# Two-layer gated trunk: feed-forward part with a right-side pool for the first gated block and every third weight slab

## The chip, the cores and the metric

The kernel runs on one NeuronCore of a Trainium2 chip. The metric is the device time of one execution in microseconds (us). The time before is the median of three runs, 2985.6 us. The page and the trace are of one further execution of the same kernel, taken by the profiler.

## What is computed

A decoder trunk of two layers on x of 1024 positions by 1024 channels, all in fp32. Of each layer, only the last lines concern the change (`attention_and_conv` stands for the rest):

```python
c_act = jax.nn.silu(c)
for l in range(2):
    mod = c_act @ ada_w[l] + ada_b[l]            # 6 vectors of 1024: shift, scale, gate, twice
    x = attention_and_conv(x, mod)
    h2 = rms_norm(x, norm2_g[l]) * (1.0 + scale2) + shift2
    f_gate, f_up = jnp.split(h2 @ w_ffn_in[l], 2, axis=-1)      # 1024 -> 2 x 2816
    x = x + (1.0 + gate2) * ((jax.nn.silu(f_gate) * f_up) @ w_ffn_out[l])   # 2816 -> 1024
return rms_norm(x, final_g)
```

## The kernel before

**Layout.** x is held transposed, eight tiles `xs[j]` of 128 channels by 1024 positions; positions are worked on in two halves of 512 (`HS`). Every operand of a matmul is split into two parts, hi and lo: ACT casts it to the matmul type (hi), and POOL or DVE subtracts hi from it (lo). One product of a 128 x 128 weight block with a 128 x 512 block is then three matmuls, hi by hi, hi by lo and lo by hi. `split_into` does the two steps; its subtraction runs on the engine that it is given, V for DVE or G for POOL.

**Feed-forward, first matrix.** It is worked in 22 groups (`Group`, FT = 22), one for each 128 columns of gate and of up. A group computes a 2 x 2 arrangement (two halves of the channels by two halves of the positions) by seven products instead of eight, each of 12 matmuls of 128 x 512. The seven right operands `MV[1]` to `MV[7]` (b1 to b7, each with h and l) are made once a layer: b1, b2, b3 in `normed`, and b4 to b7 from sums and differences of the halves of `xs` (lines 822 to 835). Each operand is four 128 x 512 blocks. The weights come as `wraw` and `fraw`, 512 KB each; sums of them are formed on DVE (lines 866 to 869, `s1`), and their split is on ACT and POOL (`wt`). The gated results go to DRAM, as `gf`. The first three groups are interleaved so that the products of b1 and b2 run while the other operands are being made; the third group's first half comes early (`r1e`).

**Second matrix.** `xs` is loaded again from `xm` (line 996), since the pool of the first `xs` was closed after the preparation. `gblock` loads four of the 22 `gf` tiles for one half of the positions as `gs` (line 970) and splits them into `gh` and `gl`; there are six blocks a half, five of four tiles and one of two. 48 slabs of weights follow (`wslab`: load at line 137, cast at 141, POOL's subtraction at 142), 24 for each half of the positions: a slab holds two columns of output by one block, 24 matmuls (lines 1017 to 1019). In layer 0 the second layer's `ada_w` is multiplied in the same stretch, 48 columns in two loads of 256 KB each (`ada_next`, `adraw`, line 987; its product on DVE is line 988); the tag `gs` has five buffers for gs, adraw and cb.

**What sets the order.** The instructions are written through a framework that puts them into an order of its own, from an estimate of each engine's time, and adds the waits. Pools of SBUF are stacks on a left and on a right side; a tile in a new pool waits for the readers of whatever lay there before. All loads and stores go through one queue, SP, in order: where one has to wait, those behind it wait too.

Of the kernel before, what the change touches and what calls it, by code (L numbers as in the profile page):

```python
# [9 lines left out]
F32 = mybir.dt.float32  # L10
# [3 lines left out]
ALU = mybir.AluOpType  # L14
# [4 lines left out]
P = 128  # L19
D = 1024  # L20
T = 1024
L = 2
KT = D // P
HF = 512
HEADS = 4
D_FF = 2816
FT = D_FF // P
# [34 lines left out]
def trunk(tc, a):  # L62
# [4 lines left out]
    def pool(name, bufs=1, side="left", **k):  # L67
        return tc.tile_pool(name=name, bufs=bufs, side=side, reuse_waits="tile", **k)
# [255 lines left out]
    def hunit(name, pl=None, tag="H", bufs=8):  # L324

        return (pl or hp).tile([P, 4, HF], F32R, tag=tag, name=name, bufs=bufs)
# [213 lines left out]
    for l in range(L):  # L540
# [240 lines left out]

        def split_into(hi, lo, src, E):
            S.copy(hi, src)  # L783
            E.tensor_tensor(lo, src, hi.bitcast(F32), op=ALU.subtract)  # L784

        HS = [slice(hf * HF, hf * HF + HF) for hf in range(2)]
        MV = {}

        def normed(hf, pb, j):

            p = {(0, 0): 1, (0, 1): 2, (1, 1): 3}.get((hf, j // 4))
            if p and p not in MV:
                MV[p] = [(hunit if hf else h2unit)(f"b{p}{n}") for n in "hl"]
            x = xs[j][:, HS[hf]]
            t = nt("ntt")
            V.scalar_tensor_tensor(t, x, acol[l][1][:, j:j + 1], pb, op0=ALU.mult, op1=ALU.mult)
            S.activation(x, t, AF.Identity, bias=modb[l][:, 24 + j:25 + j])
            if p:
                split_into(MV[p][0][:, j % 4, :], MV[p][1][:, j % 4, :], x, V if hf and j % 2 else G)

        pb = None
        for hf in range(2):
# [19 lines left out]
        for jj in range(4):  # L822
            a11, a12 = (xs[jj][:, h] for h in HS)
            a21, a22 = (xs[4 + jj][:, h] for h in HS)
            E = (V, G)[jj % 2]
            E.tensor_tensor(a11, a12, a11, op=ALU.subtract)
            E.tensor_tensor(a12, a22, a12, op=ALU.subtract)
            E.tensor_tensor(a22, a22, a11, op=ALU.subtract)
        for p, x0, h in ((6, 4, 1), (7, 0, 1), (5, 0, 0), (4, 4, 0)):
            MV[p] = [(h2unit if p == 4 else hunit)(f"b{p}{n}") for n in "hl"]  # L830
            for jj in range(4):
                x = xs[x0 + jj][:, HS[h]]
                if p == 4:
                    (G, V)[jj % 2].tensor_tensor(x, xs[4 + jj][:, HS[1]], x, op=ALU.subtract)
                split_into(MV[p][0][:, jj, :], MV[p][1][:, jj, :], x, V if jj % 2 else G)
        xpool.close()


        def bank(name):
# [5 lines left out]
        class Group:  # L845
# [9 lines left out]

            def load(self):
                r1 = wp.tile([P, D], F32, tag="wraw", name="wraw", bufs=2)
                r2 = F.tile([P, D], F32, tag="fraw", name="fraw", bufs=2)
                DQ.dma_start(r1, a["w_ffn_in"][l, self.f])
                DQ.dma_start(r2, a["w_ffn_in"][l, FT + self.f])  # L860
                self.a11, self.a12, self.a21, self.a22 = r1[:, 0:HF], r1[:, HF:D], r2[:, 0:HF], r2[:, HF:D]
# [72 lines left out]

        wtags = itertools.cycle(("wh", "wl"))
        banks = itertools.cycle((psct, p1, psct, p1, psct, pct, pmt, pmt))
        gs = [Group(f) for f in range(FT)]
        for g in gs[:2]:
            g.load()
# [7 lines left out]
        for g in gs[2:]:  # L947
            g.load()
            for p in (1, 2, 6, 7, 5, 3, 4)[2 if g is gs[2] else 0:]:
                g.product(p)  # L950
        fst.close()


# [1 line left out]
        xp = xpool.enter_context(pool(f"y{l}", side="right"))  # L955
        xs = [xp.tile([P, T], F32, tag=f"x{j}", name=f"x{j}") for j in range(KT)]
        gst = ExitStack()
        GP = gst.enter_context(pool("gbuf"))
        g2 = gcol[l][1]
        NB = (FT + 3) // 4  # L960

        def gblock(hf, b):
            if b == NB - 1:
                u = hunit("gt", GP, "G", 9)
                un = [u[:, 0:2, :], u[:, 2:4, :]]
            else:
                un = [hunit(f"g{n}") if b >= 3 + hf else hunit(f"g{n}", GP, "G", 9) for n in "hl"]
            for k in range(4 * b, min(4 * b + 4, FT)):
                t = GP.tile([P, HF], F32, tag="gs", name="gs", bufs=5)
                DQ.dma_start(t, gf[k][:, HS[hf]])  # L970
                split_into(un[0][:, k % 4, :], un[1][:, k % 4, :], t, V if k % 2 else G)
            return un

        if l + 1 < L:
            cs1 = GP.tile([P, D], F32, name="cs1", bufs=1)
            for h in HS:
                cb = GP.tile([P, HF], F32, tag="gs", name="cb", bufs=5)
                DQ.dma_start(cb, a["cb"][:, h])
                S.activation(cs1[:, h], cb, AF.Sigmoid)
                V.tensor_tensor(cs1[:, h], cs1[:, h], cb, op=ALU.mult)  # L980

        def ada_next(t):

            m2 = small("m2", 2)
            for h in range(2):
                raw = GP.tile([P, HF], F32, tag="gs", name="adraw", bufs=5)
                DQ.dma_start(raw, a["ada_w"][l + 1, t][:, HS[h]])
                V.scalar_tensor_tensor(raw, raw, 1.0, cs1[:, HS[h]], op0=ALU.mult, op1=ALU.mult,
                                       accum_out=m2[:, h:h + 1])
            m = modb[l + 1][:, t:t + 1]  # L990
            V.scalar_tensor_tensor(m, m2[:, 0:1], m2[:, 1:2], vcol(l + 1, t), op0=ALU.add, op1=ALU.add)
            ada_use(l + 1, t)

        gb = [[gblock(0, b) for b in range(NB)], []]
        for j in range(KT):
            DQ.dma_start(xs[j], xm[j])
        ada_t = iter(range(48 if l + 1 < L else 0))
        for hf in range(2):
            hs = HS[hf]
            Sq = nt("Sq")  # L1000
            for jq in range(2):
                js = range(4 * jq, 4 * jq + 4)
                pss = [(psct, psct, psct, pmt, pmt, p1, p1, pct)[j]("pfo") for j in js]
                last = hf and jq
                steps = [(b, q) for b in range(NB) for q in range(2)]
                if last:
                    steps = [(b, q) for q in range(2) for b in reversed(range(NB))]
                seen = [0, 0]
                for b, q in steps:
                    k0, k1 = 4 * b, min(4 * b + 4, FT)  # L1010
                    wh, wl = wslab(a["w_ffn_out"][l, js[2 * q]:js[2 * q] + 2, :, k0 * P:k1 * P], k1 - k0, nj=2)
                    bh, bl = gb[hf][b]
                    for jj in range(2):
                        ps = pss[2 * q + jj]
                        for k in range(k0, k1):
                            wc = slice((jj * (k1 - k0) + k - k0) * P, (jj * (k1 - k0) + k - k0 + 1) * P)
                            PE.matmul(ps, wh[:, wc], bh[:, k % 4, :], start=(not seen[q] and k == k0), stop=False)  # L1017
                            PE.matmul(ps, wh[:, wc], bl[:, k % 4, :], start=False, stop=False)  # L1018
                            PE.matmul(ps, wl[:, wc], bh[:, k % 4, :], start=False,  # L1019
                                      stop=(seen[q] == NB - 1 and k == k1 - 1))  # L1020
                    seen[q] += 1
                    for t in itertools.islice(ada_t, 3):
                        ada_next(t)
                    if hf == 0 and q == 1 and (b == 0 if jq == 0 else b < NB - 1):
                        gb[1].append(gblock(1, len(gb[1])))
                    if seen[q] == NB:
                        for j in js[2 * q:2 * q + 2]:
                            V.scalar_tensor_tensor(xs[j][:, hs], pss[j % 4], g2[:, j:j + 1], xs[j][:, hs],  # L1028
                                                   op0=ALU.mult, op1=ALU.add)
                            sum_sq(Sq, xs, hf, j)  # L1030
                            if l + 1 < L:
                                DQ.dma_start(xd[j][:, hs], xs[j][:, hs])
            pb = rstd_bcast(Sq, 1.0 / D, 1e-6, "prn")
            if l + 1 < L:
                hs_parts[hf] = norm_half(xs, hf, pb, acol[l + 1][0], modb[l + 1][:, 0:8], "h")
            else:
                for j in range(KT):
                    y = nt("y")
                    V.scalar_tensor_tensor(y, xs[j][:, hs], vec[:, FG + j:FG + j + 1], pb,  # L1039
                                           op0=ALU.mult, op1=ALU.mult)  # L1040
                    DQ.dma_start(a["out"][j][:, hs], y)
        gst.close()
    xpool.close()
    top.close()

# [55 lines left out]
```

## Time and profile before

| what | value |
|---|---|
| median of three runs | 2985.6 us (2981.32 to 2988.03) |
| profiled execution | 2990.07 us, span 2988.2 us, mean granted clock 0.965 |
| busy, of the span | PE 93%, DVE 61%, POOL 58%, ACT 39% |
| DMA | 353.92 MB, mean 118 GB/s |

The profile is read in stages, since a share of the whole span says little about any of them. In layer 0 the feed-forward's start is 793.30 to 873.50 us of the span, its steady groups run to 1251.30, the out part's first half to 1426.98 and the second half to 1550.10. In layer 1 the same borders are 2254.10, 2332.80, 2711.30 and, at the end of the out part, 2972.40.

### The profile page before, as it was taken

To read this page: it belongs to the slowest core of one execution; us is meant where nothing else is said; L and a number is where in the kernel's file an instruction comes from. 1 tells how busy PE (TensorE), PEld (TensorE's weight loads), DVE (VectorE), ACT (ScalarE), POOL (GpSimd) and SP (SyncE) were. 2 spreads that over 40 slices of the span, in tenths; PEclk is the share of its full clock that TensorE was granted. 3 is DMA by queue.
4 is the path that set the end of the run, shared out by engine and by line. 5 is a ranking of instruction groups with operands and counts; after the bars stand their busy time and mean duration, and the time that the engine had idled before them with its cause. 6 is when DMAs were issued, how large, how long until landed. Compare 5 with 4: busy or idle time off the path is not lost. (4 is left out here: it accounts for less than half of the span.)

```text
span 2988.2 us, 35455 instructions
## 1 busy us (share of the span) xinstructions
PE 2783.1 (93%) x12544; PEld 2284.7 (76%) x12544; DVE 1836.9 (61%) x2997; ACT 1158.0 (39%) x2059; POOL 1719.9 (58%) x1256
## 2 busy tenths in 40 slices
PE   3899999899979999889899999998997999998998
PEld 2688788777758888667788888886875788886886
DVE  8889976554574466589618989545446644443222
ACT  4246544343433333332322565435334233333321
POOL 6957745334686666554542776642457666666643
PEclk9999999989989999999999999998998999999999
DMA  7621222335232222388432122132451322225442
GB/s 272 229 83 65 71 78 85 113 102 194 100 110 88 78 85 85 112 277 287 158 121 89 64 75 78 56 107 85 141 201 68 119 85 85 85 78 180 136 121 93
DMA packets 151952, 353.92 MB, mean 118 GB/s; under 512 B 15328, under 2 KB 28000, under 8 KB 151776
## 3 DMA queue, kind: packets, MB, share of 16 engines
q1 hardware_dynamic: 151776, 351.67, 34.7%
q8 instruction: 99, 1.62, 0.2%
q14 instruction: 77, 0.63, 0.1%
HBM read 282.30 MB, written 69.30 MB: 118 GB/s over the span
## 5 line engine op out<-in xcount | busy, mean ns | idle before, releaser
L142 POOL TENSOR_TENSOR wl<-wraw,wh 128x1024 fp32r<-128x1024 f32 (+1 forms) x216 | 513.0, 2376 | 587.1 <-ACT wh L141 391.2
L141 ACT CAST wh<-wraw 128x1024 fp32r<-128x1024 f32 (+1 forms) x216 | 219.5, 1017 | 404.5 <-PE pfo L1018 186.7
L784 POOL TENSOR_TENSOR wt<-wraw,wt 128x512 fp32r<-128x512 f32 x172 | 247.7, 1441 | 169.6 <-ACT wt L783 169.5
L1017 PE MATMUL pfo<-gh,wh 128*128 128x512 f32 x640 | 256.1, 402 | 31.1 <-ACT gh L783 22.8
L151 PE MATMUL pg<-hl,wh 128*128 128x512 f32 x640 | 253.0, 397 | 16.9 <-DVE hl L536 16.8
L614 DVE SCALAR_TENSOR_TENSOR pc<-uc,vec,pc 128x512 f32<-128x512 f32 x348 | 261.1, 750 | 6.0
L150 PE MATMUL pg<-hh,wh 128*128 128x512 f32 x640 | 253.8, 401 | 9.1 <-ACT hh L535 8.9
L1018 PE MATMUL pfo<-gl,wh 128*128 128x512 f32 x640 | 254.3, 397 | 0.0
L1019 PE MATMUL pfo<-gh,wl 128*128 128x512 f32 x640 | 243.0, 399 | 8.7 <-POOL wl L142 8.6
L783 ACT CAST wt<-wraw 128x512 fp32r<-128x512 f32 x172 | 106.9, 622 | 310.2 <-PE pf L883 259.2
L609 POOL TENSOR_TENSOR uc<-uc,ct 128x512 f32<-128x512 f32 x120 | 139.0, 1158 | 57.5 <-ACT ct L608 56.8
L1017 PEld LDWEIGHTS pfo<-gh,wh 128*128 128x128 f32 x640 | 124.1, 194 | 60.9 <-ACT gh L783 23.7
L154 PE MATMUL pg<-hh,wl 128*128 128x512 f32 x640 | 168.7, 395 | 0.0
L443 ACT ACTIVATE e<-psc,nb 128x512 f32<-128x512 f32 (+2 forms) x192 | 110.5, 579 | 145.9 <-DVE nb L440 113.1
L1019 PEld LDWEIGHTS pfo<-gh,wl 128*128 128x128 f32 x640 | 123.3, 193 | 42.1 <-POOL wl L142 16.5
L151 PEld LDWEIGHTS pg<-hl,wh 128*128 128x128 f32 x640 | 121.0, 189 | 44.2 <-DVE hl L536 21.1
L150 PEld LDWEIGHTS pg<-hh,wh 128*128 128x128 f32 x640 | 121.8, 191 | 33.5 <-ACT hh L535 9.4
L1028 DVE SCALAR_TENSOR_TENSOR x<-pfo,gcol,x 128x512 f32<-128x512 f32 x32 | 23.7, 745 | 196.0 <-PE pfo L1019 195.5
L1018 PEld LDWEIGHTS pfo<-gl,wh 128*128 128x128 f32 x640 | 123.2, 192 | 25.9
L154 PEld LDWEIGHTS pg<-hh,wl 128*128 128x128 f32 x640 | 117.5, 188 | 23.3
L784 POOL TENSOR_TENSOR wt<-fraw,wt 128x512 fp32r<-128x512 f32 x88 | 118.7, 1349 | 26.9 <-ACT wt L783 26.9
L438 DVE TENSOR_REDUCE mx<-psc 128x1 f32<-128x512 f32 (+2 forms) x192 | 102.7, 549 | 23.8 <-PE psc L437 16.0
(324 smaller groups left out, 7652.3 us busy)
## 6 DMA issues: line engine op xcount, KB each, us to landing
wraw<-in_w_ffn_out_dram SPq DMA_DIRECT2D x80, 512.0 KB
wraw<-in_w_in_dram SPq DMA_DIRECT2D x72, 512.0 KB
adraw<-in_ada_w_dram SPq DMA_DIRECT2D x48, 512.0 KB
adraw<-in_ada_w_dram SPq DMA_DIRECT2D x96, 256.0 KB
fraw<-in_w_ffn_in_dram SPq DMA_DIRECT2D x44, 512.0 KB
wraw<-in_w_ffn_in_dram SPq DMA_DIRECT2D x44, 512.0 KB
gs<-gf SPq DMA_DIRECT2D x88, 256.0 KB
gd<-graw SPq DMA_DIRECT2D x64, 256.0 KB
```

The lines of the kernel that those rows point to most:

```text
L141: S.copy(wh, raw)
L142: G.tensor_tensor(wl, raw, wh.bitcast(F32), op=ALU.subtract)
L150: PE.matmul(ps, wh[:, wc], rhs(0, k, hf), start=(k == 0), stop=False)
L151: PE.matmul(ps, wh[:, wc], rhs(1, k, hf), start=False, stop=False)
L154: PE.matmul(ps, wl[:, wc], rhs(0, k, hf), start=False, stop=(k == nk - 1))
L443: S.activation(e[:, n0:n1], pss[b][:, 0:n1 - n0], AF.Exp, bias=nb, scale=0.125, accum_out=sx[:, 2 * b + c:2 * b + c + 1])
L609: G.tensor_tensor(acc, acc, t, op=ALU.add)
L614: E.scalar_tensor_tensor(pc if k + 1 < CONV_K else acc, u[:, k:k + HF], w, pc, op0=ALU.mult, op1=ALU.add)
L784: E.tensor_tensor(lo, src, hi.bitcast(F32), op=ALU.subtract)
L1017: PE.matmul(ps, wh[:, wc], bh[:, k % 4, :], start=(not seen[q] and k == k0), stop=False)
L1018: PE.matmul(ps, wh[:, wc], bl[:, k % 4, :], start=False, stop=False)
L1019: PE.matmul(ps, wl[:, wc], bh[:, k % 4, :], start=False, stop=(seen[q] == NB - 1 and k == k1 - 1))
```

## The change

- A pool `ffnr` (R) is opened on the right side when the first `xs` pool has been closed, and stays until the layer's end. It holds one buffer for the second slab of every third group (`rraw`), the hi and lo parts of one gated block (`G0`), and the five gs buffers; `cs1` uses rraw's place later. The G tag falls from 9 to 7 buffers.
- The first gated block of the first half, `gblock(0, 0)`, is written into the feed-forward groups, behind group FT - 4; `gblock` itself moves ahead of the groups.
- The reloads of `xs` from `xm` move from ahead of the out part's slabs to its first steps.
- `ada_next` is called once a step, where it was called three times.
- Of the preparation, every subtraction of the second half of the positions, the differences and their splits go to DVE, where they alternated between DVE and POOL.

```diff
@@ normed
-                split_into(MV[p][0][:, j % 4, :], MV[p][1][:, j % 4, :], x, V if hf and j % 2 else G)
+                split_into(MV[p][0][:, j % 4, :], MV[p][1][:, j % 4, :], x, V if hf else G)
@@ differences
-            E = (V, G)[jj % 2]
+            E = V
             E.tensor_tensor(a11, a12, a11, op=ALU.subtract)
             E.tensor_tensor(a12, a22, a12, op=ALU.subtract)
             E.tensor_tensor(a22, a22, a11, op=ALU.subtract)
...
-                    (G, V)[jj % 2].tensor_tensor(x, xs[4 + jj][:, HS[1]], x, op=ALU.subtract)
-                split_into(MV[p][0][:, jj, :], MV[p][1][:, jj, :], x, V if jj % 2 else G)
+                    V.tensor_tensor(x, xs[4 + jj][:, HS[1]], x, op=ALU.subtract)
+                split_into(MV[p][0][:, jj, :], MV[p][1][:, jj, :], x, V)
         xpool.close()
+        rst = ExitStack()
+        R = rst.enter_context(pool("ffnr", side="right"))
@@ Group.load
-                r2 = F.tile([P, D], F32, tag="fraw", name="fraw", bufs=2)
+                if self.f % 3 == 2:
+                    r2 = R.tile([P, D], F32, tag="rraw", name="rraw", bufs=1)
+                else:
+                    r2 = F.tile([P, D], F32, tag="fraw", name="fraw", bufs=2)
@@ gblock (moved ahead of the groups)
+            if b == NB - 1:
+                u = hunit("gt", GP[0], "G", 7)
+                un = [u[:, 0:2, :], u[:, 2:4, :]]
+            elif b == 0 and hf == 0:
+                un = [hunit(f"g{n}", R, "G0", 2) for n in "hl"]
+            elif b == 1 and hf == 1:
+                un = [hunit(f"g{n}", R, "G0", 2) for n in "hl"]
+            else:
+                un = [hunit(f"g{n}") if b >= 3 + hf else hunit(f"g{n}", GP[0], "G", 7) for n in "hl"]
+            for k in range(4 * b, min(4 * b + 4, FT)):
+                t = R.tile([P, HF], F32, tag="gs", name="gs", bufs=5)
@@ groups
             for p in (1, 2, 6, 7, 5, 3, 4)[2 if g is gs[2] else 0:]:
                 g.product(p)
+            if g.f == FT - 4:
+                gb = [[gblock(0, 0)], []]
@@ out part
-        gb = [[gblock(0, b) for b in range(NB)], []]
-        for j in range(KT):
-            DQ.dma_start(xs[j], xm[j])
+        gb[0] += [gblock(0, b) for b in range(1, NB)]
...
-                    for t in itertools.islice(ada_t, 3):
+                    for t in itertools.islice(ada_t, 1):
                         ada_next(t)
+                    if hf == 0 and jq == 0 and q == 0 and b >= 2:
+                        for j in range(2 * b - 4, 2 * b - 2):
+                            DQ.dma_start(xs[j], xm[j])
```

The order of both kernels shows what becomes of this on the engines. The lines of the changed file are a few higher: 864 and 865 are the loads of wraw and of fraw or rraw (859 and 860 before), 871 to 874 the weight sums (866 to 869), 957 the load of gs (970), 1000 that of adraw (987), 1037 that of x from xm (996).

First, DVE at the end of the preparation in layer 0; b4l is the lo part of the last operand, s1 the first weight sum of the third group. Before:

```order
L784 TENSOR_TENSOR b6l_7134<-x7_6416,b6h_7133 128x512
L784 TENSOR_TENSOR b4l_7164<-x7_6416,b4h_7163 128x512
L915 TENSOR_TENSOR u2_7202<-pf_7352,u2_7202 128x512
L919 TENSOR_TENSOR u3_7399<-pf_7386,u2_7202 128x512
L915 TENSOR_TENSOR u2_7220<-pf_7369,u2_7220 128x512
...
L892 TENSOR_TENSOR u2_7220<-u2_7220,c22_7458 128x512
L892 TENSOR_TENSOR c11_7277<-c11_7277,u3_7417 128x512
L866 TENSOR_TENSOR s1_7512<-fraw_7508 128x512
```

And with the change:

```order
L784 TENSOR_TENSOR b6l_7134<-x5_6414,b6h_7133 128x512
L784 TENSOR_TENSOR b5l_7154<-x0_6409,b5h_7153 128x512
L784 TENSOR_TENSOR b5l_7154<-x1_6410,b5h_7153 128x512
L784 TENSOR_TENSOR b5l_7154<-x2_6411,b5h_7153 128x512
L784 TENSOR_TENSOR b5l_7154<-x3_6412,b5h_7153 128x512
L784 TENSOR_TENSOR b6l_7134<-x6_6415,b6h_7133 128x512
L784 TENSOR_TENSOR b4l_7164<-x4_6413,b4h_7163 128x512
L784 TENSOR_TENSOR b6l_7134<-x7_6416,b6h_7133 128x512
L784 TENSOR_TENSOR b4l_7164<-x5_6414,b4h_7163 128x512
L784 TENSOR_TENSOR b4l_7164<-x6_6415,b4h_7163 128x512
L784 TENSOR_TENSOR b4l_7164<-x7_6416,b4h_7163 128x512
L871 TENSOR_TENSOR s1_7515<-rraw_7511 128x512
```

All four b4l and b5l are now on DVE, and s1 follows the last b4l at once; before, 14 rows that take in the products' results stood between the two.

Second, SP at the feed-forward's start in layer 0, behind the first weight loads. Before:

```order
L859 DMA wraw<-in_w_ffn_in_dram 128x1024 x2
L996 DMA x_10333<-xm 128x1024
L996 DMA x_10334<-xm 128x1024
L996 DMA x_10335<-xm 128x1024
L996 DMA x_10336<-xm 128x1024
L996 DMA x_10337<-xm 128x1024
L860 DMA fraw<-in_w_ffn_in_dram 128x1024
```

And with the change:

```order
L864 DMA wraw<-in_w_ffn_in_dram 128x1024 x2
L865 DMA rraw<-in_w_ffn_in_dram 128x1024
L865 DMA fraw<-in_w_ffn_in_dram 128x1024 x2
L898 DMA gf<-c_7259 128x512
L898 DMA gf<-u_7205 128x512
L898 DMA gf<-c_7280 128x512
L957 DMA gs<-gf 128x512
```

The eight loads of x are gone from this place, the third group's second slab (rraw) stands ahead of the next two groups', and the first load of the gated block follows the third store.

Third, SP at the start of layer 0's out part. Before, from the fourth slab's load:

```order
L137 DMA wraw<-in_w_ffn_out_dram 128x2x512
L978 DMA cb<-in_cb_dram 128x512 x2
L970 DMA gs<-gf 128x512 x22
L137 DMA wraw<-in_w_ffn_out_dram 128x2x512
L987 DMA adraw<-in_ada_w_dram 128x512 x3
```

And with the change, again from the fourth slab's:

```order
L137 DMA wraw<-in_w_ffn_out_dram 128x2x512
L1037 DMA x_10354<-xm 128x1024
L1037 DMA x_10355<-xm 128x1024
L1037 DMA x_10356<-xm 128x1024
L1037 DMA x_10357<-xm 128x1024
L1037 DMA x_10358<-xm 128x1024
L957 DMA gs<-gf 128x512 x4
L1037 DMA x_10359<-xm 128x1024
L957 DMA gs<-gf 128x512
L1037 DMA x_10360<-xm 128x1024
L1037 DMA x_10361<-xm 128x1024
L137 DMA wraw<-in_w_ffn_out_dram 128x2x512 x2
```

Between the fourth and the fifth slab there were 22 loads of gs (and cb); there are now eight of x, of twice the size, and five of gs. Up to slab 28 the order before holds 96 loads of adraw and 30 of gs, counted from the first slab on; the new one 59 and 35 to 37, the others of gs standing in the feed-forward groups.

## Rows read from the trace of the kernel before

**Rows 1.** The page: each engine's busy time, share of the span, instructions.

```profile
PE 2783.1 (93%) x12544; PEld 2284.7 (76%) x12544; DVE 1836.9 (61%) x2997; ACT 1158.0 (39%) x2059; POOL 1719.9 (58%) x1256
```

**Rows 2.** Stages: from:to, length, busy of PE, PEld, DVE, ACT, POOL, clock, DMA share, GB/s.

```profile
793.30:873.50 80.20, 56.87 (x209) 41.31 (x207) 57.92 (x59) 33.33 (x58) 60.81 (x42) 0.81 0.27 98
873.50:1251.30 377.80, 377.72 (x1656) 312.31 (x1656) 215.34 (x255) 118.70 (x197) 246.64 (x178) 0.99 0.23 81
1251.30:1426.98 175.68, 145.59 (x577) 115.14 (x577) 145.58 (x296) 48.41 (x65) 81.97 (x42) 0.89 0.84 277
1426.98:1550.10 123.12, 117.25 (x497) 95.24 (x498) 45.97 (x53) 38.27 (x52) 60.61 (x30) 0.96 0.42 130
2254.10:2332.80 78.70, 54.91 (x210) 39.96 (x208) 57.87 (x59) 33.20 (x58) 60.82 (x42) 0.86 0.28 99
2332.80:2711.30 378.50, 378.49 (x1656) 312.78 (x1656) 188.88 (x253) 120.80 (x197) 242.50 (x178) 0.99 0.24 81
2711.30:2972.40 261.10, 247.56 (x1072) 201.00 (x1072) 72.39 (x67) 77.98 (x105) 139.61 (x71) 0.97 0.45 138
```

**Rows 3.** Timeline of PE, layer 0's start: start, us, operation, [idle before, what ended it].

```profile
825.32 0.50 PE L881 MATMUL pf<-b3l,wt 128*128 128x512 f32 x1 [2.29 <-DVE b3l L784]
...
839.87 0.79 PE L881 MATMUL pf<-b6l,wt 128*128 128x512 f32 x1 [6.11 <-POOL b6l L784]
...
873.54 0.79 PE L880 MATMUL pf<-b7h,wt 128*128 128x512 f32 x1 [5.81 <-ACT wt L783]
```

**Rows 4.** Timeline of DVE, the same stretch.

```profile
825.19 1.77 DVE L827 TENSOR_TENSOR x<-x,x 128x512 f32<-128x512 f32 x1
...
858.68 1.78 DVE L784 TENSOR_TENSOR b4l<-x,b4h 128x512 fp32r<-128x512 f32 x1
860.38 0.68 DVE L915 TENSOR_TENSOR u<-pf,u 128x512 f32<-128x512 f32 x1
...
871.33 0.68 DVE L866 TENSOR_TENSOR s<-fraw 128x512 f32<-128x512 f32 x1
```

**Rows 5.** Timeline of POOL, the same stretch: two rows of its own work.

```profile
829.74 3.40 POOL L889 TENSOR_TENSOR c<-c,sg 128x512 f32<-128x512 f32 x2
...
855.25 2.96 POOL L784 TENSOR_TENSOR wt<-s,wt 128x512 fp32r<-128x512 f32 x2
```

**Rows 6.** Timeline of the SP queue: x at layer 0's start, gs at its out part.

```profile
850.33 5.78 SPq L996 DMA_DIRECT2D x<-xm  x5
...
1257.00 25.84 SPq L970 DMA_DIRECT2D gs<-gf  x22
```

**Rows 7.** Timeline of PE: the first matmuls of the out part, layers 0 and 1.

```profile
1263.28 1.22 PE L1017 MATMUL pfo<-gh,wh 128*128 128x512 f32 x2 [12.02 <-ACT gh L783]
...
2722.09 1.22 PE L1017 MATMUL pfo<-gh,wh 128*128 128x512 f32 x2 [10.80 <-ACT gh L783]
```

**Rows 8.** DMA view from 1251.30 to 1426.98: total, and issues with their size.

```profile
DMA packets 26794, 48.58 MB, mean 277 GB/s; under 512 B 2617, under 2 KB 3641, under 8 KB 26783
...
adraw<-in_ada_w_dram SPq DMA_DIRECT2D x96, 256.0 KB
...
gs<-gf SPq DMA_DIRECT2D x32, 256.0 KB
```

**Rows 9.** Shorter stretches of the out parts, columns as in rows 2.

```profile
1300.00:1400.00 100.00, 92.43 (x376) 73.32 (x375) 92.20 (x210) 20.47 (x25) 41.53 (x19) 0.93 0.86 285
1350.00:1355.00 5.00, 5.00 (x23) 4.13 (x22) 4.96 (x14) 1.05 (x1) 1.86 (x1) 1.00 0.99 356
2720.00:2725.00 5.00, 2.91 (x7) 2.33 (x8) 2.08 (x2) 3.09 (x5) 2.79 (x2) 0.50 0.66 235
```

**Rows 10.** Attention and projections in layers 0 and 1, columns as in rows 2.

```profile
165.90:611.20 445.30, 427.68 (x2138) 357.15 (x2136) 341.77 (x691) 224.48 (x508) 257.54 (x236) 0.97 0.23 79
1638.90:2071.40 432.50, 419.39 (x2137) 352.50 (x2136) 311.87 (x660) 225.69 (x508) 256.43 (x235) 0.98 0.23 80
```

More of the change, by code (lines that the diff above doesn't have):

```diff
@@ L936, in trunk, with gblock @@
         banks = itertools.cycle((psct, p1, psct, p1, psct, pct, pmt, pmt))
+        GP = [None]
+        NB = (FT + 3) // 4
+        def gblock(hf, b):
+            if b == NB - 1:
[9 more added lines that the diff above has]
+                t = R.tile([P, HF], F32, tag="gs", name="gs", bufs=5)
+                DQ.dma_start(t, gf[k][:, HS[hf]])
+                split_into(un[0][:, k % 4, :], un[1][:, k % 4, :], t, V if k % 2 else G)
+            return un
         gs = [Group(f) for f in range(FT)]
@@ L957, in trunk @@
         gst = ExitStack()
-        GP = gst.enter_context(pool("gbuf"))
+        GP[0] = gst.enter_context(pool("gbuf"))
         g2 = gcol[l][1]
[L960 to L972, printed above, removed]
         if l + 1 < L:
-            cs1 = GP.tile([P, D], F32, name="cs1", bufs=1)
+            cs1 = R.tile([P, D], F32, tag="rraw", name="cs1", bufs=1)
             for h in HS:
-                cb = GP.tile([P, HF], F32, tag="gs", name="cb", bufs=5)
+                cb = R.tile([P, HF], F32, tag="gs", name="cb", bufs=5)
                 DQ.dma_start(cb, a["cb"][:, h])
@@ L985, in ada_next @@
             for h in range(2):
-                raw = GP.tile([P, HF], F32, tag="gs", name="adraw", bufs=5)
+                raw = R.tile([P, HF], F32, tag="gs", name="adraw", bufs=5)
                 DQ.dma_start(raw, a["ada_w"][l + 1, t][:, HS[h]])
@@ L1042, in trunk @@
         gst.close()
+        xpool.close()
+        rst.close()
+        xpool = ExitStack()
     xpool.close()
```

## The prediction

> **What bounds the kernel now.** The page comes first: PE is busy for 93% of the span [rows 1], so at most 7% can be won from its idle time, and any further gain must come from matmuls run at a low clock. Next the span cut into stages, to see where that idle time lies [rows 2]. The reader is to see three sorts of stage. In the feed-forward's steady part (873.50 to 1251.30, and 2332.80 to 2711.30) PE is busy throughout at a clock of 0.99, and one product matmul costs 377.72/1656 = 0.228 us. At its start (793.30, 2254.10) PE works 56.87 of 80.20 us and 54.91 of 78.70, at 0.81 and 0.86. In its out part the first half of layer 0 has 145.59 of 175.68 at 0.89, beside 277 GB/s of DMA; the second half (123.12) and the whole of layer 1 (261.10) are nearer to PE's own pace: 528 matmuls a half are 120.4 us.
>
> Why the start is slow is read in PE's timeline: it waits for the lo parts b3l and b6l, and at its end 5.81 us for the weights of the third group [rows 3]. The makers of those parts show why: a subtraction with two SBUF inputs takes 1.77 to 1.78 us on DVE while POOL runs its own, and 0.68 where POOL has stopped (the row of s) [rows 4, 5]. The last of the preparation ends at 860.4. The out part begins, in both layers, with a wait of 12.02 and 10.80 us for gh, the first gated block [rows 7], for whose loads SP needs 25.84 us [rows 6].
>
> **The change, part by part.** The sum is made against the profiled execution, 2990.07 us (span 2988.2), which lies 4.5 above the median of the runs, 2985.6; the forecast is then given on the median.
>
> *Start of the feed-forward, per layer.* All 36 two-input operations of the preparation go to DVE; before, DVE and POOL did 18 each. POOL keeps what else it did between 826 and 860: three sigmoid products (1.7 each) and six weight splits (about 1.5 to 1.7) [rows 5], some 15 us. By the order, b3l's four splits end with DVE's c11 rows, about 827 as now (a second pair of splits on DVE, at 1.77 at most, for POOL's). Behind it stand one row of c11 and 30 two-input operations. Nine of them meet POOL's nine and cost 1.7 (15.3 us); 21 run alone at 0.68 (14.3): the preparation ends near 857. PE needs the last b4l for the last two products, 24 matmuls or 5.5 us, and so ends near 863 and goes on with group 3 at once: in the new order s1 stands right behind the last b4l, where it stood behind 14 result rows, and its input rraw is loaded before the preparation ends. Before, the third group started at 873.54. That is 10; I take **9**, since rraw lies where the x tiles were and its load must wait for the last reader of them. Bounds: 3 (only half of the 5.81 goes) and 15 (ten products of 12 matmuls from 827 on, at 0.228, end at 854.4; less 4 for the clock, which is 0.81 over this stage with its waits). The 18 operations taken from POOL are worth nothing by themselves: it is not waited for there but for them.
>
> *The x reloads.* Eight loads of 512 KB leave the feed-forward's start, where SP spent 5.78 us on the first five [rows 6] and held back fraw behind them; that is inside the 9. They now stand ahead of the fifth slab of the out part.
>
> *The first gated block, built during the feed-forward.* Its 4 loads, 4 casts and 4 subtractions move into the steady part, where ACT is busy for 118.70 of 377.80 us, POOL for 246.64 and DMA at 0.23 [rows 2]: nothing. Each load waits on SP for a store of gf, and what queues behind it is the weight load of a later group; a group is 377.80/20 = 18.9 us, so the wait is hidden unless it nears that. Without that cover the four subtractions on POOL would be 7 us at most.
>
> *Out part of layer 0.* Its first half is set by transfers: 48.58 MB [rows 8] in 175.68 us. Up to slab 28, which opens the second half, SP's order had 30 gs, 96 adraw and no x loads; now it has 35 gs (nine are earlier), 59 adraw, and eight x of twice the size: 110 units of 256 KB against 126. 48.58 - 16 x 0.262 = 44.4 MB, at the 285 GB/s of its steady 100 us [rows 9] 155.8 us: **19.9** less. The 37 adraw that move to the second half bring it from 123.12 us at 130 GB/s, 16.0 MB, to 25.7 at most, of some 34 that 120 us carry at 285; it stays with its matmuls, 120.4 us at best: **2** of those 2.7. The 12.02 us wait for gh is not counted beside it, since a transfer-bound half takes it in. Bounds: 10, if only that wait goes and 2 come back, and 39 (rival A).
>
> *Out part of layer 1.* No adraw. The wait of 10.80 goes, and with it about 1.5 of a PE that runs at 0.50 behind it (2.91 busy us in the row from 2720) [rows 7, 9]. A new wait comes: ahead of slab 5 now stand 16 units of x and 5 of gs; with the slab 6.0 MB, at 277 to 356 GB/s [rows 2, 9] 17 to 22 us, covered by 4 x 24 x 0.228 = 21.9 us of the first four slabs. With issue, landing and cast I charge 4, and 1.5 for the clock. Gain **7**, between 0 and 11.
>
> *Fewer G buffers (9 to 7), three adraw columns a step to one:* the buffers that left are in the right-side pool, and the columns are counted above. Layer 1's attention comes out in another order on DVE, ACT and POOL, with PE's the same. The two layers differ in that stretch by 445.30 - 432.50 = 12.8 us [rows 10]; I take 0, between -13 and +13.
>
> Sum: 9 + 9 + 22 + 7 = 47. 2990.07 - 47 = 2943; on the median 2938.6, so **2939**.
>
> **The rivals.** *A, more.* With 16 fewer units in the way, transfers run nearer to the 356 GB/s of the best stretch [rows 9], say 320: 44.4 MB then take 138.8, and layer 0 gains 39. With the starts at their bound of 15 and layer 1 at 11: 80, or 2906. For it: DMA is 0.84 to 0.86 busy, not full. Against: adraw goes through the same five gs buffers as before, and each is refilled only after DVE has read it. The Trainium skill ("DMA: Bandwidth & Descriptors", section Bandwidth) gives 341 GB/s for a transfer of 1 MB, by which an estimate of the half would be 130 us; this case's mean of 277 is below it and its best 5 us above.
>
> *B, less.* DVE's chain now does alone what two engines did, and its order puts the second b6l behind eight others: the starts win 3 each, layer 0 only 12, layer 1 only 2. Sum 20: 2966. For it: the same work is merely on one engine. Against: beside each other the pair finish two operations in 1.77, DVE alone two in 1.36.
>
> *C, slower.* POOL fills the time it wins with weight splits of its own, so that DVE never runs alone: 31 operations at 1.70 take 52.7 us, the preparation ends at 880 and not 860.4, +19.3 a layer; with 29 won in the out parts the kernel is 9.6 slower: 2995. It decides from a loss of 14.5 a layer. For it: each row of DVE's beside POOL is 1.77 or so [rows 4]. Against: POOL's splits wait for a weight buffer that PE frees, and nine operations are 15 us, not 52. The Trainium skill ("SBUF: State Buffer", section on the two separate sides) says that a DVE operation with two SBUF inputs and a POOL operation that reads SBUF hold one shared port by turns, the loser blocked for a whole instruction; the rows, 0.68 alone against 1.77, agree.
>
> *D, no change.* B's sum, with layer 1's attention 13 longer and nothing in layer 1's out part: 20 - 2 - 13 = 5. That the change doesn't do what it says is ruled out by the order rows of both kernels.
>
> **How the numbers follow.** The forecast has 0.52, A 0.16, B 0.22, C 0.06, D 0.04. Its own range is 2918 to 2960 (the starts 3 to 12 each, layer 0 12 to 30). The range given, 2900 to 2970, reaches past A and B, and leaves out C, D and the far ends. What a measurement can tell from no change is about 0.2%, or 6 us: faster 0.90 (forecast, A, B), same 0.04 (D), slower 0.06 (C).
>
> **What would show it.** In the changed profile: the stretch from the first group's products to the third group's is about 71 us instead of 80 and 79; DVE's last b4l ends near 857 on that scale, most of its rows near 0.68; the wait for gh in front of the out part is gone; the first half of layer 0's out part is about 156 us with 16 units less moved, and the second 121; a wait of some 4 us stands at the fifth slab in layer 1. The prediction is wrong if DVE's rows stay at 1.77 (C), if the first half stays near 170 us though its units fell (B), or if a store of gf holds SP so long that weight loads come late in the steady part.

## The result and the profile after

The changed kernel takes 2955.46 us (median of four runs, 2953.43 to 2956.81), the kernel before 2985.82 in the same comparison: ratio 0.990, 95% interval 0.9882 to 0.9917. It is faster by 30 us, inside the range and not the 47 that were forecast. Its profiled execution is 2956.39 us, span 2954.6. The page's busy times:

```profile
PE 2780.6 (94%) x12544; PEld 2281.2 (77%) x12544; DVE 1874.8 (63%) x3033; ACT 1150.6 (39%) x2059; POOL 1676.9 (57%) x1220
```

PE does the same work; its idle time in the span fell from 205 to 174 us. Where these 31 us lay is read from the same stages as in [rows 2], with the same columns. The borders are again the first matmul of the feed-forward, the point where the third group's second part begins (209 or 210 matmuls lie ahead of it, as before), the end of the groups, in layer 0 PE's first matmul of the first half's sum of squares, and the end of the out part:

```profile
791.27:857.70 66.43, 53.27 (x210) 40.82 (x209) 55.21 (x73) 32.70 (x58) 35.26 (x23) 0.87 0.13 47
857.70:1235.84 378.14, 376.54 (x1658) 310.52 (x1656) 223.06 (x263) 121.88 (x206) 250.15 (x182) 1.00 0.26 90
1235.84:1411.77 175.93, 146.10 (x574) 113.49 (x572) 115.72 (x197) 50.77 (x72) 92.57 (x47) 0.92 0.73 248
1411.77:1536.37 124.60, 119.58 (x499) 95.30 (x500) 69.57 (x148) 30.54 (x37) 53.23 (x26) 0.96 0.56 179
2238.70:2307.40 68.70, 56.10 (x209) 43.11 (x208) 55.73 (x73) 32.25 (x57) 34.61 (x23) 0.83 0.14 45
2307.40:2684.70 377.30, 376.26 (x1657) 310.67 (x1656) 222.60 (x260) 120.96 (x204) 248.51 (x182) 1.00 0.25 89
2684.70:2938.42 253.72, 247.60 (x1073) 200.53 (x1071) 74.54 (x64) 74.82 (x100) 139.12 (x69) 0.99 0.47 149
```

| stage | before | after | forecast of the gain | gain |
|---|---|---|---|---|
| start, layer 0 | 80.20 | 66.43 | 9 | 13.8 |
| start, layer 1 | 78.70 | 68.70 | 9 | 10.0 |
| steady groups, both layers | 756.3 | 755.4 | 0 | 0.9 |
| out part, layer 0 | 298.80 | 300.53 | 22 | -1.7 |
| out part, layer 1 | 261.10 | 253.72 | 7 | 7.4 |

Each figure is of one execution, and the same stage can differ by some 3 us from one to another: run 1 below, whose out part in layer 0 is that of before, has 295.9 there. So the -1.7 can't be told from no gain, but it is far from 22. The five make 30.4 of the 33.6 us of span; the rest lies before the two starts, where nothing but the order on the engines differs.

*The start.* DVE's timeline at the end of layer 0's preparation, to be read beside [rows 4]:

```profile
839.67 2.48 DVE L784 TENSOR_TENSOR b5l<-x,b5h 128x512 fp32r<-128x512 f32 x4
842.08 0.68 DVE L784 TENSOR_TENSOR b6l<-x,b6h 128x512 fp32r<-128x512 f32 x1
...
843.88 1.89 DVE L784 TENSOR_TENSOR b4l<-x,b4h 128x512 fp32r<-128x512 f32 x3
```

Four splits with two SBUF inputs take 2.48 us, 0.62 each: alone, DVE starts the next 0.6 us after the last. The preparation ends at 845.77, 54.5 after the stage's first matmul; before it was 860.46 - 793.30 = 67.2. The wait of 5.81 us for the third group is gone.

*The out parts.* The waits of 12.02 and 10.80 us for gh [rows 7] are gone. At the fifth slab stands the new wait that the prediction charged with 4 us, here the first matmul of that slab in layer 0 and in layer 1 (timeline of PE):

```profile
1263.88 0.80 PE L1028 MATMUL pfo<-gh,wh 128*128 128x512 f32 x1 [5.78 <-ACT wh L141]
...
2711.42 0.80 PE L1028 MATMUL pfo<-gh,wh 128*128 128x512 f32 x1 [4.46 <-ACT wh L141]
```

In layer 1 the sum comes out. In layer 0 it does not, though the transfers fell as forecast; the DMA view of the first half, beside 48.58 MB at 277 GB/s before [rows 8]:

```profile
DMA packets 22951, 43.67 MB, mean 248 GB/s; under 512 B 2195, under 2 KB 3219, under 8 KB 22940
```

4.9 MB less are carried in the same time, at a lower rate. Nor is 285 GB/s the most that the transfers reach here: the same view gives the rate in 40 slices of 4.4 us, and four in a row, where x and gs are loaded, have 389 to 410, one among loads of adraw 358:

```profile
GB/s 51 206 397 397 410 389 221 168 248 240 122 294 347 136 274 312 290 336 358 293 291 162 196 202 274 180 67 246 275 168 172 272 259 148 264 316 208 290 206 244
```

The cast of a slab (ACT, line 141) places the loss. Before, those of slabs 5 and 28:

```profile
1287.96 1.06 ACT L141 CAST wh<-wraw 128x1024 fp32r<-128x1024 f32 x1 [2.08 <-PE pfo L1018]
...
1428.21 1.04 ACT L141 CAST wh<-wraw 128x1024 fp32r<-128x1024 f32 x1 [4.45 <-DMA wraw<-in_w_ffn_out_dram]
```

And after, the same two slabs:

```profile
1262.78 1.05 ACT L141 CAST wh<-wraw 128x1024 fp32r<-128x1024 f32 x1 [3.44 <-DMA wraw<-in_w_ffn_out_dram]
...
1414.55 1.05 ACT L141 CAST wh<-wraw 128x1024 fp32r<-128x1024 f32 x1 [6.40 <-PE pfo L1029]
```

From the end of the groups to slab 5 it was 36.7 us (1251.3 to 1287.96) and is 26.9 (1235.84 to 1262.78): 9.8 won. From slab 5 to slab 28 it was 140.3 and is 151.8: 11.5 lost. What a slab waits for there is seen at slabs 20 and 21. First the timeline of SP, then that of POOL, whose subtraction frees the slab's buffer (there are two buffers):

```profile
1344.06 1.42 SPq L1000 DMA_DIRECT2D adraw<-in_ada_w_dram  x3
1350.69 4.04 SPq L957 DMA_DIRECT2D gs<-gf  x4
1354.99 0.33 SPq L1000 DMA_DIRECT2D adraw<-in_ada_w_dram  x1
1355.42 0.90 SPq L137 DMA_DIRECT2D wraw<-in_w_ffn_out_dram  x2
```

```profile
1347.73 5.15 POOL L142 TENSOR_TENSOR wl<-wraw,wh 128x1024 fp32r<-128x1024 f32 x2 [4.25 <-ACT wh L141]
```

POOL frees the two buffers at about 1350.1 and 1352.9; SP issues both loads only at 1355.42, since it stands before four gs and an adraw that wait for one of five gs buffers. That is 5.3 and 3.0 us after the buffer was free. Taken so for slabs 5 to 28 (a slab's issue on SP less the end of POOL's subtraction two slabs earlier), the mean is 2.87 us before and 4.03 after, and 0.14 and 0.61 in layer 1, where no adraw stands in the queue. Slabs 5 and 6, right behind the loads of x, have 8.3 and 4.8 of it (7.0 and 3.5 in layer 1); without these two the mean rises from 2.9 to 3.8. From issue to cast it is 6.00 before and 6.14 after. Two buffers go round in this loop, so a slab's pitch, the time from one cast to the next, rises by about half of what is added, from 6.10 to 6.60 us.

So there were two theories: **bytes**, the prediction's own (the half is set by what the transfers carry, now at a lower rate), and **queue** (it is set by how long a slab's load stands on SP behind loads that wait for the gs buffers).

### The profile page after: what moved, and what is told of

Read it like the earlier page. It is cut to its first block, busy times and chain, and to the rows that moved or that the text cites. A ratio compares the mean times of both kernels' runs of the same rounds, so it can differ in the third digit from the quotient of the medians.

```text
span 2954.6 us, 35366 instructions
## 1 busy us (share of the span) xinstructions
PE 2780.6 (94%) x12544; PEld 2281.2 (77%) x12544; DVE 1874.8 (63%) x3033; ACT 1150.6 (39%) x2059; POOL 1676.9 (57%) x1220
## 5 line engine op out<-in xcount | busy, mean ns | idle before, releaser
L784 POOL TENSOR_TENSOR wt<-wraw,wt 128x512 fp32r<-128x512 f32 x172 | 237.8, 1386 | 149.9 <-ACT wt L783 148.1
L479 POOL TENSOR_TENSOR ss<-ss,nhalf 128x1 f32<-128x1 f32 x64 | 37.9, 592 | 136.8 <-DVE ss L478 136.3
```

## The experiments

A ratio is to the kernel before, measured beside the run (2986 to 2989 us); the changed kernel's own is 0.990, 0.9882 to 0.9917. SP's delay of a slab and its pitch are worked out as above, for slabs 5 to 28 of layer 0. The border between the halves lies behind 556 to 576 matmuls of the out part, by the run, so that halves compare to within some 5 us only; the whole out part is free of that.

**1. The preparation alone.** The kernel before, with:

```diff
-                split_into(MV[p][0][:, j % 4, :], MV[p][1][:, j % 4, :], x, V if hf and j % 2 else G)
+                split_into(MV[p][0][:, j % 4, :], MV[p][1][:, j % 4, :], x, V if hf else G)
...
-            E = (V, G)[jj % 2]
+            E = V
...
-                    (G, V)[jj % 2].tensor_tensor(x, xs[4 + jj][:, HS[1]], x, op=ALU.subtract)
-                split_into(MV[p][0][:, jj, :], MV[p][1][:, jj, :], x, V if jj % 2 else G)
+                    V.tensor_tensor(x, xs[4 + jj][:, HS[1]], x, op=ALU.subtract)
+                split_into(MV[p][0][:, jj, :], MV[p][1][:, jj, :], x, V)
```

> The kernel before with one part of the change alone: all second-half subtractions, differences and splits of the preparation on DVE. If DVE alone is what shortens the feed-forward's start, the last b4l ends some 12 us earlier in both layers, and the third group starts 7 to 12 us earlier than before: 14 to 24 us in all, 2962 to 2972. If the rest of the start's gain comes from the x reloads and the third slab's own buffer, the third group still waits for its weight sums behind the result rows and for fraw: under 3 us a layer, 2980 or more.

2976.4 us, ratio 0.9955 (0.994 to 0.997). The two starts:

```profile
790.29:862.80 72.51, 53.71 (x209) 40.98 (x207) 56.84 (x78) 32.82 (x58) 35.40 (x24) 0.88 0.29 108
2238.52:2310.50 71.98, 53.38 (x210) 40.59 (x208) 56.88 (x78) 32.82 (x58) 35.81 (x24) 0.88 0.30 108
```

7.7 and 6.7 us, the lower edge of what was expected for the first case; the total is 12.7 us below the kernel before. But the third group still waits, as the second case had it (timeline of PE):

```profile
862.83 0.80 PE L880 MATMUL pf<-b7h,wt 128*128 128x512 f32 x1 [5.47 <-ACT wt L783]
```

**2. All but the preparation.** The changed kernel with those four edits undone.

> The changed kernel with the preparation shared by DVE and POOL again. The preparation alone gave 7.7 and 6.7 us at the two starts when it was put into the kernel before; the whole change gave 13.8 and 10.0. If the parts add up, the starts are 74 to 76 us here and the total is 12 to 17 above the changed kernel: 2966 to 2972. If the x reloads and the third slab's buffer are worth nothing once the preparation is slow, the starts are back at 78 to 80, total 2975.

2972.72 us, ratio 0.9955 (0.9938 to 0.9972). The starts are 72.73 and 74.30, 7.5 and 4.4 below before, and the wait for the third group is gone. With run 1 that is 15.2 and 11.1, against 13.8 and 10.0 for the whole: the two parts of the start are worth about as much each, add up nearly, and the steady groups are some 3 to 4 us longer in each layer (381.3 and 381.8). The two ratios multiply to 0.991. Which of three things takes the wait away, the x reloads gone, the third slab's own buffer or the new order on DVE, was not tried.

**3. The slabs' loads from ACT.**

```diff
-            DQ.dma_start(raw.rearrange("p (j k) -> p j k", j=nj), src.rearrange("j p k -> p j k"))
+            (S if sq else DQ).dma_start(raw.rearrange("p (j k) -> p j k", j=nj), src.rearrange("j p k -> p j k"))
```

> The changed kernel with the out part's weight slabs loaded through ACT's queue, so that they no longer stand behind gs and adraw on SP. Theory queue (a slab's load waits on SP behind loads that wait for one of five gs buffers; bytes are not the limit): the first half of layer 0's out part falls from 176 to 130 to 150 us, total 2925 to 2940. Theory bytes (the half is limited by what the transfers carry, at 248 GB/s now): it stays within 5 us of 176, total 2950 to 2960, unless ACT's casts are held up by the loads' waits, which would show as longer waits for wh.

2958.82 us, ratio 0.9899 (0.9884 to 0.9913): no gain. Theory queue missed by 19 us, and the first half stays at 175.6, where theory bytes had it. The slab's delay fell from 4.03 to 2.35, but issue to cast rose from 6.14 to 7.82. ACT is a queue too: it now stands before casts of gh whose gs is late, 40.9 us in all (27.1 in the changed kernel), as the view of waits has it for the first half:

```profile
ACT gh L783 <- DMA gs<-gf: 40.9, 9, 9.6
```

The run does not decide between the theories: the wait changed its engine.

**4. Three adraw columns a step again**, in the changed kernel.

> The changed kernel with three adraw columns a step again, as before the change. Up to slab 28 the order then holds 84 adraw and 28 gs instead of 59 and 44. Theory bytes: 9 loads of 256 KB more than the changed kernel at 248 GB/s, about +10 us in the first half, total 2960 to 2970. Theory queue: what counts is how close behind each other the loads of the five-buffer ring and the slabs stand; without the late gs loads among the slabs the first half is no longer than now, 165 to 178 us, total 2945 to 2958.

2953.87 us, ratio 0.9878 (0.9862 to 0.9895). The first half is 165 us and the second 136:

```profile
1242.40:1407.50 165.10, 144.06 (x576) 113.23 (x576) 125.53 (x260) 41.55 (x55) 76.87 (x38) 0.93 0.83 278
1407.50:1543.30 135.80, 119.62 (x497) 95.45 (x496) 54.38 (x85) 40.11 (x54) 65.46 (x36) 0.92 0.46 147
```

More adraw in the first half, and it is 11 us shorter: theory bytes expected 10 longer. The delay is 3.42. What was won is lost in the second half, which is 11 us longer; 14 of the gs loads went there (by the DMA view the first half has 84 adraw and 21 gs, 62 and 35 in the changed kernel). Between one and three columns a step the out part does not differ (300.9 against 300.5).

**5. No adraw at all.** The changed kernel with neither the 96 loads nor their products.

> The changed kernel without the 96 loads of adraw and their products (the second layer's modulation is left at its bias and a constant). Both theories: the first half of layer 0's out part falls to between 122 and 135 us, since about 28 MB are left and DVE frees each gs buffer sooner; what remains above 120 is the wait at the fifth slab, 5.8 us now. Total 2905 to 2918. If the first half stays above 150, neither adraw's bytes nor its buffers set it, but the order of x, gs and slabs alone.

2914.8 us, ratio 0.9753 (0.9738 to 0.9768).

```profile
1238.80:1379.60 140.80, 132.68 (x564) 106.21 (x564) 54.18 (x38) 51.35 (x74) 91.51 (x48) 0.98 0.62 204
1379.60:1494.70 115.10, 114.26 (x510) 94.10 (x509) 30.63 (x34) 30.63 (x37) 53.15 (x27) 1.00 0.36 108
```

The out part is 256, like layer 1's; adraw costs the changed kernel 44.6 us there. The slab's delay is 0.63 and the pitch 5.12, close to PE's own (528 matmuls in 24 slabs, 5.02 us each). From issue to cast it is 6.83, but here only 6 of the 24 casts wait last for their load, the others for PE or for ACT's own work. The first half was expected at 122 to 135: too low, since 564 matmuls, more than 528, lie ahead of its border.

**6. The loads without their products.** The changed kernel, SP's order nearly the same, each gs buffer free as soon as its adraw has landed:

```diff
-                V.scalar_tensor_tensor(raw, raw, 1.0, cs1[:, HS[h]], op0=ALU.mult, op1=ALU.mult,
-                                       accum_out=m2[:, h:h + 1])
...
-            V.scalar_tensor_tensor(m, m2[:, 0:1], m2[:, 1:2], vcol(l + 1, t), op0=ALU.add, op1=ALU.add)
+            V.scalar_tensor_tensor(m, cs1[:, 0:1], cs1[:, 1:2], vcol(l + 1, t), op0=ALU.add, op1=ALU.add)
```

> The changed kernel with all 96 loads of adraw in nearly the same places of SP's order, but without their products on DVE (the second layer's modulation is left at its bias and a constant). The bytes are those of the changed kernel; a gs buffer comes free when its load has landed, not when DVE has read it. Theory bytes: the first half of layer 0's out part stays between 170 and 176 us and the out part at 295 or more. Theory queue, by the buffers' turn: SP's delay of a slab falls from 4.0 us by what DVE's part of the turn is; first half 145 to 165, out part 262 to 285, total 2920 to 2942.

2930.28 us, ratio 0.9811 (0.9797 to 0.9826).

```profile
1239.10:1399.20 160.10, 139.30 (x564) 109.64 (x564) 49.89 (x38) 51.43 (x74) 90.11 (x48) 0.93 0.82 285
1399.20:1514.10 114.90, 114.34 (x511) 94.13 (x510) 30.74 (x34) 30.64 (x38) 53.10 (x27) 1.00 0.56 181
```

The same loads pass at 285 and not 248 GB/s, and the out part is 275: 25 us less with not a byte less to load. The delay is 2.37, the pitch 5.96. **Theory bytes falls here.** Of adraw's 44.6 us some 25 hang on its products, which hold a gs buffer and stand in DVE's queue, and 19 on the loads. A third reading, that DVE's products slow the subtraction on POOL which frees a slab's buffer, explains little: a full slab's subtraction takes 2.57 us in the changed kernel and 2.48 here. The runs don't part the products' hold on a buffer from the time that they take of DVE, nor do they say what makes up the 19; the rate that is left, 285 GB/s, is the one that the prediction took for the limit, but slices of this half too reach 385 to 406.

**7 and 8. adraw's loads from ACT, and from POOL** (`S.dma_start` and `G.dma_start` in `ada_next`).

> The changed kernel with the loads of adraw alone issued from ACT, so that on SP a slab stands behind gs loads only. Theory queue: SP's delay of a slab falls to 1 to 2 us, but ACT, which makes wh and gh, now stands before the buffers that DVE frees; if its waits are short, the out part of layer 0 is 270 to 290 and the total 2925 to 2945; if ACT's queue takes over the delay, as it did when the slabs were issued there, the out part stays at 298 to 303.

> As the run before, with the loads of adraw issued from POOL, whose own work in the out part is the wl subtraction of each slab (2.4 us of some 6.2). Theory queue: SP is free of the buffers that DVE frees; a slab's buffer is freed by POOL's wl, and any wait of POOL before an adraw load comes into the same loop. Out part of layer 0 between 275 and 305; total 2930 to 2958.

From ACT: 2955.79 us, ratio 0.9898 (0.9883 to 0.9913), out part 304; the delay falls to 2.21, issue to cast rises to 8.29. From POOL: **2944.23 us, ratio 0.9858 (0.9842 to 0.9875)**, faster than the changed kernel, whose interval begins at 0.9882. Its two halves:

```profile
1239.10:1400.80 161.70, 139.98 (x557) 110.25 (x555) 110.20 (x166) 49.73 (x70) 114.74 (x96) 0.92 0.73 251
1400.80:1528.40 127.60, 121.57 (x517) 97.09 (x518) 86.56 (x179) 31.92 (x39) 78.52 (x74) 0.97 0.61 198
```

The delay is 1.83 and the pitch 6.23. The Trainium skill ("DMA: Bandwidth & Descriptors", section Issuing engines are not separate DMA queues) says that issuing from several engines saves only the time that it takes to initiate a transfer, usually little. Here the choice of engine is worth 11 us of out part, or nothing, by what waits behind the load, which is more than the time to initiate. On ACT the casts of every slab stand behind the load.

**9. Own buffers for adraw**, two, and three for gs in layer 0, in place of five shared.

> The changed kernel with two buffers of its own for adraw and three for gs in layer 0, in place of five shared. By the order, 18 of the 96 loads now stand in the feed-forward groups and 74, not 59, ahead of slab 28. Theory queue: SP waits in either case for the older load's reader; with two buffers the wait for DVE is longer for each adraw, so the out part does not fall below 295; if sharing was the fault (gs behind adraw's products), it falls to 275 to 290, total 2930 to 2945.

2963.37 us, ratio 0.9922 (0.9907 to 0.9936). The first half is 185.7, the out part 308, as theory queue had it: sharing was not the fault. That fewer buffers for each kind make it longer isn't shown alone, since the loads' places moved with them, and the interval overlaps the changed kernel's.

**10 and 11. adraw in the steady groups**, two and three columns a group; the call of `ada_next` moves behind a group's products, and rraw is left to `cs1` from the third group on:

```diff
+            if g.f > 2:
+                for t in itertools.islice(ada_t, 2):
+                    ada_next(t)
...
-                if self.f % 3 == 2:
+                if self.f % 3 == 2 and (l + 1 == L or self.f == 2):
```

> The changed kernel with 38 of the 48 adraw columns moved into layer 0's steady feed-forward groups, two a group from the fourth on, through the right-side pool's gs buffers; the silu of c sits in rraw's place from the third group on, so that later groups use fraw alone in that layer. Theory queue (each slab of the out part loses some 4 us between its free buffer and its issue, because SP stands before loads of the five gs buffers): the out part of layer 0 falls from 300.6 us towards the 256 of the run without adraw, 258 to 275; the steady groups, with DMA at 0.26 and DVE at 219.76 of 374.84 us busy, grow by 0 to 10. Total 2918 to 2935. If DVE's queue in the steady part is held up by products whose loads are late, the steady part grows by 20 or more and the total stays above 2940.

> As the run before, with three columns a group, so that all 48 lie in the steady groups. Theory queue: the out part of layer 0 falls to 254 to 262, the steady part grows by 0 to 15; total 2910 to 2930. If the five gs buffers are too few in the steady part, for gblock's loads stand in the same ring, the steady part pays 20 or more.

2957.1 us (0.9903, 0.9889 to 0.9918) and 2958.88 (0.9909, 0.9894 to 0.9924). The out part falls as theory queue said, to 267 and 256; the steady groups pay it all back, 411.6 and 421.5 us against 378.1. No load of adraw is waited for by DVE there, so late loads of adraw do not hold up its queue. Late weights do: in the run with two columns DVE waits in these groups for fraw (view of waits),

```profile
DVE s L871 <- DMA fraw<-in_w_ffn_in_dram: 53.4, 12, 6.2
```

In the changed kernel DVE waits 38.0 us for weights there, at most 3.5 at a time, and PE hardly for what follows from them (1.0 us for wt from ACT, against 19.4). SP stands 50.0 us before loads of adraw whose buffer DVE's product still holds: that looks like the same fault in another place. How much is SP's order, how much the lost third buffer, rraw, and how much DVE's added work (306.58 us busy against 223.06) wasn't tried.

**12. The first block without its place in the right-side pool.**

> The changed kernel without G0: the first gated block goes into the G buffers of the left side again (9 of them), while gs, rraw and the rest stay in the right-side pool. Its loads may still begin in the feed-forward, its split parts have no place before the feed-forward's buffers are free. If the place of gh is what took the wait at the out part's beginning away, a wait of 4 to 12 us is back in both layers; in layer 1 the out part is 5 to 9 us longer. In layer 0 theory queue says that the loss shows in full, up to 10 us; theory bytes that it does not show. Total 2960 to 2972.

2954.18 us, ratio 0.9896 (0.9881 to 0.9911), the same as the changed kernel and 6 us below what was expected. In layer 1 the first half is 144.3 us, where the changed kernel has 138.8 and the one before 146.8: there G0 brings most of the gain. In layer 0 PE waits for gl instead of gh (timeline of PE),

```profile
1242.23 0.50 PE L1023 MATMUL pfo<-gl,wh 128*128 128x512 f32 x1 [3.45 <-POOL gl L784]
...
1244.46 0.80 PE L1023 MATMUL pfo<-gl,wh 128*128 128x512 f32 x1 [0.97 <-DVE gl L784]
```

but not at the fifth slab, and its out part is 297.7, no longer than the changed kernel's (run 2, whose out part is the same as that one's, has 297.5). What layer 1 loses the steady groups give back: they are 375.5 us in each layer, and 377 to 379 in the changed kernel and in the other runs that build the block early, as far as adraw stays in the out part and the preparation on DVE. The expected loss in layer 0 did not show, which theory queue had to show in full: a miss for it as it was stated then.

## Why the prediction came out as it did

*The direction and the range were right*; the size of 47 was too large by one term of 22 in layer 0. That the total still came out at 30 is in part luck: the starts gave 6 us more than forecast and the stretches before them 3 that nobody forecast. 2955 lies nearer to rival B's 2966 than to 2939, and inside the range because the range reached past B. B's reason did not hold, though: the starts won 13.8 and 10.0 and not 3 each. The lower end of the forecast's own range, 2918, does not follow from its terms either: starts of 12 each, 30 in layer 0 and 7 in layer 1 make 61, or 2925.

*The starts, 9 and 9: right in kind, too small.* 13.8 and 10.0, inside the bounds of 3 and 15. The 21 operations that run alone were costed at 0.68, the duration of a row; DVE starts one every 0.6 us. Nine were costed at 1.7 against POOL's nine, but the timeline has two single rows of 1.76 and a pair of 2.35 in that stretch: only three of POOL's operations run in its first part, and the next two, begun at 842.53, take 5.63 us, where such a pair took 2.96 before [rows 5]. Runs 1 and 2 show that the other half of the gain is the third group's wait, which the prediction booked with the first. The Trainium skill ("SBUF — State Buffer", section SBUF: two separate sides) has DVE and POOL block each other for whole instructions where DVE's has two SBUF inputs and POOL's reads SBUF; 1.77 us beside POOL and 0.62 alone agree with that.

*Layer 1's out part, 7: right*, 7.4, with 4.46 us at the fifth slab where 4 was charged.

*The first block built early, at no cost to the steady groups: nearly right.* They differ from before by at most 1.2 us a layer, but run 12, without the early block, has them 2 to 3 us shorter, so that the block seems to cost that much and another part of the change to cover it.

*Layer 0's out part, 20 and 2: wrong, -1.7.* The step that failed is "Its first half is set by transfers". The prediction's own sign of being wrong came true, "if the first half stays near 170 us though its units fell": it is 175.93. The bytes fell as worked out (43.67 MB, where 44.4 were forecast), but the rate of 285 GB/s was an outcome and not a limit: with DVE's products gone and the loads kept, the out part is 25 us shorter (run 6). The row that the rate was taken from held another reading: in the same 100 us DVE is busy for 92.20 [rows 9], most of it with adraw's products. One takes 0.68 us when POOL is still and up to 2.84 beside a subtraction of POOL's (timeline of DVE, 1340.68); the mean is 0.975 (view of lines, kernel before, 1283 to 1425):

```profile
L988 DVE SCALAR_TENSOR_TENSOR adraw<-adraw,cs 128x512 f32<-128x512 f32 x93 | 89.4, 975 | 9.2 <-DMA adraw<-in_ada_w_dram 8.5 <-DVE adraw L988 0.4
```

So before the change the reader of the buffers was itself close to full; with the change it is busy for 115.72 of 175.93 us, and the half is no shorter. In the place of the transfers stands a loop of two slab buffers, into which SP's wait for the gs buffers enters. Where the change took adraw out it let in 16 units of x and more gs; each gs holds its buffer until ACT and then POOL or DVE have split it. The 9.8 us won at the beginning went into a delay of 4.03 us a slab. "The 37 adraw that move to the second half" do not stay hidden either: it rose by 1.5 where 2 were to be won. That DMA had room there (25.7 MB of 34) was no evidence, for the same reason: with the loads and without their products this half is 114.9 us (run 6), with neither 115.1 (run 5), and with both 124.6.

*The rivals.* A (transfers faster) falls with the same step. B's price for layer 0, "only 12", was too high as well. C is refuted: most of DVE's rows are 0.68, and POOL did not fill the time, its busy time in the stage fell from 60.81 to 35.26 us.

Open stays why three arrangements (before, changed, three columns a step) give the same 299 to 301 us of out part in layer 0. Which part of the added delay is the gs loads, which the x loads and which the G tag's seven buffers wasn't tried.

## What to carry to other kernels

A stretch with 280 GB/s and DMA at 0.85 looks limited by transfers. Keep the loads and take away what reads them: if it gets shorter, the bytes were not the limit, and the readers' own time, the buffers that they hold and the queue that waits for those buffers come into question. Then look at the load that the bottleneck engine needs, and measure from its buffer's release to its issue; a load that waits for a slow reader should not stand in front of it on an in-order queue. Moving either to another engine helped here only where less that was urgent stood behind it: on POOL, not on ACT.

Work split between DVE and POOL gained nothing here, where each operation is on 128 x 512 in fp32 with two SBUF inputs: a pair costs 1.77 us side by side, and two on DVE alone 1.24.

## What was not expected of the hardware

The time from a slab's issue to its cast did not grow with the traffic beside it: 6.0 to 6.1 us among adraw loads at 248 to 277 GB/s, 6.8 without any at 204. This is not the time of the transfer: in it lie the waits of the cast for PE and for ACT's own work. Of the 24 casts 15 wait last for their load before, 13 in the changed kernel and 6 without adraw. So the figures do not show that a transfer takes no longer in traffic.

POOL could issue adraw's loads without becoming the bound: in the first half its busy time rises from 92.57 us (47 rows) to 114.74 (96 rows), 0.45 us for each row more, while the whole out part gets 11 us shorter.
